# Attention output by stationary values: two heads in the halves of one bank, reciprocal sums turned and spread by small products

## The chip, the cores and the metric

The kernel runs on one core of a Trainium2 chip. The metric is the device time of one execution in microseconds (us). The engines of the core work side by side, each from its own queue, in order: TensorE (PE) multiplies matrices and writes only to PSUM, VectorE (DVE), ScalarE (ACT) and GpSimd (POOL) do the rest, and SyncE (SP) issues most of the loads. PSUM has eight banks of 128 partitions by 512 floats; the kernel uses seven as working banks and one for a convolution.

## The reference

Two layers of an encoder block on 512 tokens of 1024 features, all in float32:

```python
for l in range(DEPTH):
    x = x + 0.5 * swiglu(rms_norm(x, ffn1_norm[l]), ...)
    h = rms_norm(x, mix_norm[l])
    p = h @ w_in[l]
    attn = mla_group(...)   # 8 heads, query and key width 96, value width 64
    conv = conv_group(...)  # gate, causal depthwise conv of 31 taps on 512 channels, LayerNorm, silu
    x = x + jnp.concatenate([attn, conv], axis=-1) @ w_out[l]
    x = x + 0.5 * swiglu(rms_norm(x, ffn2_norm[l]), ...)
    x = rms_norm(x, post_norm[l])
```

In the attention each block of 128 queries sees the keys up to its own end, with a mask in steps of 64 tokens; the softmax is over the keys, and a head's output is the softmax's weights times the values:

```python
probs = jax.nn.softmax(scores, axis=-1)
outs.append(jnp.einsum('bhqk,bhkd->bqhd', probs, vs))
```

## The kernel before

Activations are kept with the features on the partitions and the 512 tokens along the free axis (x is eight tiles of 128 by 512). The large products run in three passes on split operands: each float is a rounded high part and a remainder, and `mm3` (lines 153 to 156) adds high times high, high times low and low times high. `split` (line 158) makes the two parts, the high one on ACT, the low one on DVE. The seven working banks come from `bank`, scratch tiles from `tmp` (five buffers), operands from a ring of 40 slots of 128 by 512.

A layer is FFN1, the mixer (`mix_body`), and FFN2. The mixer projects the input, builds the queries q and keys kn with the tokens on the partitions, and the values vs, four tiles of 128 tokens by 512 (eight heads of 64). Then the heads run as a software pipeline. `ORDER` lists the stages, each with its lag in steps; in a step, head (step - lag) goes through each stage:

- `turn` (line 799, lag 0) turns a head's queries and keys, so that the 96 features are on the partitions.
- `scores` (line 812, lag 1) makes the scores of four query blocks against 128, 256, 384 and 512 keys (line 825), adds the mask with a small bf16 product (line 826), takes the row maximum on DVE (line 827) and the exponential on ACT (line 831), which also leaves the row sums in `sums`: tokens on the partitions, four query blocks by two heads of a pair.
- `turn_p` (line 836, lag 3) turns the ten blocks of 128 by 128 of weights (line 846) and copies them to the ring (line 849): for each key block j a tile pt[j] with the keys on the partitions and the queries from block j to the last along the free axis.
- `values` (line 852, lag 4): for each query block t and each key block j up to t, a float32 product with the block of pt[j] stationary (128 by 128) and the head's 64 columns of vs[j] moving. The two heads of a pair share a bank; the query tokens are on its partitions. After the odd head DVE takes the reciprocals of the sums (line 864) and multiplies the bank by them (line 866), a factor for each token and head.
- `turn_out` (line 870, lag 5), for odd heads: four turns of 128 by 128 on PE (line 877) bring the pair's 128 features onto the partitions, and `split` makes one operand of the output product.

A float32 product is two matmuls in the trace; a turn is one.

The depthwise convolution runs meanwhile. Blocks 0 and 3 of its channels run on DVE (line 900), blocks 1 and 2 as products on ACT (line 904) and sums on POOL (line 908), the latter with three buffers in between. POOL then adds up the four blocks (lines 922 to 924), and PE takes the mean over the channels from that (line 926). The LayerNorm follows: DVE subtracts the mean, ACT and DVE sum the squares, PE sums over the partitions (line 192), POOL takes the inverse root (line 172), PE spreads it (line 210), DVE and ACT finish (lines 942 to 945). The output product takes four operands from the attention (`at`) and four from the convolution (`cv`); `early_groups` (line 914) does the attention's half of the first output tiles before the convolution's half is there. Four weight tiles of w_out are loaded ahead (`WOP`).

The order of each engine's queue is not the order of the program text. A planner simulates the program with its own costs of the instructions and emits each instruction when its inputs and buffers would be there, earlier program text first.

Of the kernel before, what the change touches and what calls it, by code (L numbers as in the profile page):

```python
# [7 lines left out]
FP = mybir.dt.float32  # L8
# [47 lines left out]
EVP = "DAD"  # L56
ORDER = "t0s1p3v4o5"

# [12 lines left out]
@with_exitstack  # L71
def encoder_kernel(ctx: ExitStack, tc: tile.TileContext, xT, consts, vecs, rgain, wgu1, wd1,
                   wcv, wql, wkl, wuq, wkv, wout, wgu2, wd2, wend, gend, out):
# [12 lines left out]
    def nm(s):  # L86
        uid[0] += 1
        return f"{s}{uid[0]}"
# [4 lines left out]
    def tmp(w=S, dt=FP):  # L93
        return tmps.tile([P, w], dt, tag="t", name=nm("t"))

    def bank():
        return psum.tile([P, S], FP, tag="ps", name=nm("ps"))
# [513 lines left out]
    def mix_body(kpool, l, gx, norm, done):  # L611
# [61 lines left out]


        tabs = []
        for side in range(2):
# [175 lines left out]
        def values(h):  # L852

            if h % 2 == 0:
                heads[h]["po"] = bank()
            po = heads[h - h % 2]["po"].rearrange("p (t h d) -> p t h d", t=NT, h=2)
            for t in range(NT):
                for j in range(t + 1):
                    T.matmul(po[:, t, h % 2], heads[h]["pt"][j][:, (t - j) * P:(t - j + 1) * P],  # L859
                             vs[j][:, h * DV:(h + 1) * DV], start=j == 0, stop=j == t)  # L860
            if h % 2 == 0:
                return
            rs = small.tile([P, NT, 2], FP, tag="rs", name=nm("rs"))
            V.reciprocal(rs, heads[h - 1]["sums"])
            o = tmp()
            V.tensor_tensor(o.rearrange("p (t h d) -> p t h d", t=NT, h=2), po,
                            rs[:, :, :, None].to_broadcast([P, NT, 2, DV]), ALU.mult)
            heads[h]["o"] = o

        def turn_out(h):  # L870

            if h % 2 == 0:
                return
            o = heads[h]["o"]
            ps = bank()
            for t in range(NT):
                T.transpose(ps[:, t * P:(t + 1) * P], o[:, t * P:(t + 1) * P], ident)
            at.append(split(ps))

        STAGES = [({"t": turn, "s": scores, "p": turn_p, "v": values, "o": turn_out}[c], int(d)) for c, d in zip(ORDER[::2], ORDER[1::2])]  # L880
        for step in range(H + 6):
# [277 lines left out]
```

## Time and profile before

| | before |
|---|---|
| median of three runs | 1769.82 us (1769.27 to 1770.27) |
| profiled execution | 1768.75 us |
| its span, first to last instruction | 1767.0 us |
| PE busy | 1747.5 us (99%) |
| DVE busy | 1399.8 us (79%) |
| ACT busy | 948.1 us (54%) |
| POOL busy | 266.4 us (15%) |
| line 859, values products | 320 matmuls, 39.6 us busy |
| line 877, turns of the output | 32 matmuls, 5.0 us busy |

The profiled execution is one execution recorded by the hardware's profiler; its time beside the span includes what lies around the first and the last instruction. Busy times are averages over the whole span; a matmul's recorded duration overlaps with its neighbours', so the time that a matmul holds PE is read from its start to the next one's. In the rows below a timeline gives start, duration, engine, line, operation, tiles (output, then inputs), shapes (stationary rows by columns, then the moving or the output shape), and in brackets the idle time before with what ended it. A grouped row gives the count, then busy time and mean duration in ns, then idle time and its releasers. The attention of layer 0 lies between 446 and 503 us, that of layer 1 between 1322 and 1379.

### The profile page before, as it was taken

Reading aid. Unit: us, or ns where it says so; the run is one execution under the profiler, and the core shown is the slowest. Engines: PE = TensorE matmul, PEld = TensorE weight load, DVE = VectorE, ACT = ScalarE, POOL = GpSimd, SP = SyncE. Lnnn points to the kernel's source line nnn. Section 1 sums busy time; section 2 is a strip of 40 time slices with the busy share of each in tenths; the row PEclk is TensorE's granted clock in tenths of the full one; section 3 lists DMA queues with packets and bytes.
Section 4 is the critical chain, followed back from the end, with each engine's and each line's share of the span. In section 5 each row is a group of like instructions: output and inputs, shape, how many; then the busy total and the mean of one; then the engine's idle time right before and its main releaser. Section 6 shows DMA issues by size and latency. Waiting matters only on the chain.

```text
span 1767.0 us, 22287 instructions
## 1 busy us (share of the span) xinstructions
PE 1747.5 (99%) x8166; PEld 1447.9 (82%) x8166; DVE 1399.8 (79%) x2021; ACT 948.1 (54%) x1484; POOL 266.4 (15%) x213
## 2 busy tenths in 40 slices
PE   8999999999999999999999999999999999999998
PEld 7788888888788888888888888888887888888886
DVE  8967887689869877878789778866989698678794
ACT  7535445457955544446555344444679555344453
POOL 1000000048842000000000000000578400000000
PEclk9999999999999999999999999999999999999999
DMA  9454434324225455352924445343251444444345
GB/s 294 138 178 138 153 98 138 125 78 128 52 106 132 129 159 166 102 161 85 294 86 153 134 136 162 103 136 115 73 140 26 143 105 152 162 143 144 107 135 151
DMA packets 121629, 236.72 MB, mean 134 GB/s; under 512 B 10544, under 2 KB 58032, under 8 KB 121520
## 3 DMA queue, kind: packets, MB, share of 16 engines
q1 hardware_dynamic: 117488, 222.08, 39.6%
q0 software_dynamic: 3456, 12.58, 3.9%
q8 instruction: 64, 1.05, 0.2%
q10 hardware_dynamic: 576, 0.64, 0.1%
q14 instruction: 45, 0.37, 0.1%
HBM read 207.99 MB, written 25.17 MB: 132 GB/s over the span
## 4 chain that ended last, share of the span: by engine, by line
PE 89%; DVE 3%; DMA 2%; POOL 2%; issue 2%; ACT 1%; SPq 1%; POOLq 0%; DVEq 0%; ACTq 0%
PE ps L154 28%; PE ps L156 28%; PE ps L155 28%; PE ps L859 2%; PE ps L825 2%; POOL y L908 1%; DMA fr<-in_wgu 1%; PE ps L846 1%; DMA d<-e 1%; DVE wl L241 1%; PE ps L192 0%; DMA r<-d 0%; PE ps L802 0%; PE ps L807 0%; POOL wl L149 0%
## 5 line engine op out<-in xcount | busy, mean ns | idle before, releaser
L155 PE MATMUL ps<-wl,r 128*128 128x512 f32 (+2 forms) x1434 | 548.3, 384 | 1.9 <-DVE wl L241 1.9
L156 PE MATMUL ps<-wh,r 128*128 128x512 f32 (+2 forms) x1434 | 544.4, 383 | 0.0
L154 PE MATMUL ps<-wh,r 128*128 128x512 f32 (+2 forms) x1434 | 529.1, 384 | 2.6 <-ACT wh L406 1.6
L239 ACT CAST wh<-fr 128x1024 fp32r<-128x1024 f32 x255 | 267.6, 1052 | 235.0 <-PE ps L155 111.1
L156 PE MATMUL ps<-r,wl 128*128 128x512 f32 x944 | 366.2, 390 | 0.5 <-POOL wl L149 0.5
L155 PE MATMUL ps<-r,wh 128*128 128x512 f32 x944 | 366.2, 390 | 0.0
L154 PE MATMUL ps<-r,wh 128*128 128x512 f32 x944 | 362.4, 393 | 1.3 <-ACT r L396 0.9
L241 DVE TENSOR_TENSOR wl<-fr,wh 128x1024 fp32r<-128x1024 f32 x255 | 309.9, 1218 | 50.2 <-ACT wh L239 49.6
L155 PEld LDWEIGHTS ps<-wl,r 128*128 128x128 f32 x1434 | 269.2, 188 | 55.3 <-DVE wl L241 3.7
L154 PEld LDWEIGHTS ps<-wh,r 128*128 128x128 f32 x1434 | 269.0, 188 | 54.8 <-ACT wh L406 1.9
L156 PEld LDWEIGHTS ps<-wh,r 128*128 128x128 f32 x1434 | 269.1, 188 | 51.7 <-issue 0.2
L143 ACT CAST wh<-raw 128x1024 fp32r<-128x1024 f32 (+2 forms) x142 | 139.8, 989 | 214.8 <-PE ps L155 87.7
L154 PEld LDWEIGHTS ps<-r,wh 128*128 128x128 f32 x944 | 177.1, 188 | 41.2 <-ACT r L396 2.0
L155 PEld LDWEIGHTS ps<-r,wh 128*128 128x128 f32 x944 | 177.2, 188 | 38.5 <-issue 1.4
L156 PEld LDWEIGHTS ps<-r,wl 128*128 128x128 f32 x944 | 177.2, 188 | 38.3 <-POOL wl L149 1.3
L149 DVE TENSOR_TENSOR wl<-raw,wh 128x1024 fp32r<-128x1024 f32 (+3 forms) x126 | 145.7, 1158 | 70.8 <-ACT wh L143 68.1
L908 POOL TENSOR_TENSOR y<-y,pr 128x511 f32<-128x511 f32 (+14 forms) x120 | 158.0, 1317 | 53.6 <-ACT pr L904 46.6
L338 DVE TENSOR_TENSOR fr<-fr,fr 128x1024 f32<-128x1024 f32 x112 | 136.3, 1218 | 10.8 <-DMA fr<-in_wgu 10.8
L486 DVE TENSOR_TENSOR x<-ps,x 128x512 f32<-128x512 f32 x120 | 81.6, 686 | 57.3 <-PE ps L156 56.9
L172 POOL TENSOR_TENSOR rtok<-vtok,minus_half 128x4 f32<-128x4 f32 x8 | 10.4, 1304 | 750.5 <-DVE vtok L198 750.5
L368 ACT ACTIVATE e<-e,rtok 128x256 f32<-128x256 f32 x120 | 59.8, 507 | 78.2 <-DVE e L359 77.8
L397 DVE TENSOR_TENSOR r<-r,r 128x512 fp32r<-128x512 f32 x88 | 58.2, 680 | 45.5 <-ACT r L396 45.4
(198 smaller groups left out, 1772.7 us busy)
## 6 DMA issues: line engine op xcount, KB each, us to landing
fr<-in_wgu SPq DMA_DIRECT2D x175, 512.0 KB, 4.1
raw<-in_wd SPq DMA_DIRECT2D x56, 512.0 KB, 4.5
d<-e SPq DMA_DIRECT2D x176, 128.0 KB, 3.0
r<-d SPq DMA_DIRECT2D x88, 256.0 KB, 3.7
raw<-in_wd SPq DMA_DIRECT2D x32, 384.0 KB, 4.1
raw<-in_wcv SPq DMA_DIRECT2D x16, 512.0 KB, 3.2
raw<-in_wout SPq DMA_DIRECT2D x16, 512.0 KB, 3.6
raw<-in_wgu SPq DMA_DIRECT2D x8, 512.0 KB, 8.2
```

Source lines behind the costliest of these rows:

```text
L143: A.copy(hi[:, :w], raw[:, :w])
L149: (G if kind in POOLW.split() else V).tensor_tensor(lo[:, :w], raw[:, :w], hi[:, :w].bitcast(FP), ALU.subtract)
L154: T.matmul(o, lh, rh, start=first, stop=False, skip_group_check=free)
L155: T.matmul(o, lh, rl, start=False, stop=False, skip_group_check=free)
L156: T.matmul(o, ll, rh, start=False, stop=last, skip_group_check=free)
L239: order["cast"] = A.copy(hi[:, :w], src[:, :w]).ins
L241: V.tensor_tensor(lo[:, :w], src[:, :w], hi[:, :w].bitcast(FP), ALU.subtract)
L338: V.tensor_tensor(oh, ah, bh, ALU.add)
L368: A.activation(out[j][:, :h], src[j][:, :h], AF.Silu, scale=r)
L397: V.tensor_tensor(d, d.bitcast(FP), hi.bitcast(FP), ALU.subtract)
L486: V.tensor_tensor(xm, pd.rearrange("p (a t j) -> p t a j", a=4, t=NT), xm, ALU.add)
L908: order["conv"] = G.tensor_tensor(acc[:, s:], acc[:, s:], pr[:, s:], ALU.add).ins
```

## The change

The values products are done for both heads of a pair in the odd head's step. The head's 64 columns of vs[j] are now stationary and pt[j] is moving, all its 512, 384, 256 or 128 queries at once; the even head's result goes to partitions 0 to 63 of the bank, the odd head's to 64 to 127. The bank then has features on its partitions already, so `turn_out` and its stage are gone. The factor that belongs to a token now runs along the free axis. To get it there, the reciprocal sums (128 tokens by 8) are turned on PE, copied by DVE to SBUF (8 by 128), and four small float32 products with constant 0/1 tiles of 8 by 128 (`sel`, one per query block, loaded once in each layer) spread each head's row over that head's 64 partitions in a second bank. ACT copies this bank to SBUF, DVE multiplies the values bank by it, and `split` now reads the product from SBUF instead of PSUM.

```diff
--- before.py
+++ after.py
@@ -54,7 +54,7 @@
 WOG = 3
 WOP = 4
 EVP = "DAD"
-ORDER = "t0s1p3v4o5"
+ORDER = "t0s1p3v4"
 
 VECS = [("g1", 8), ("gm", 8), ("g2", 8), ("gp", 8), ("gql", 3), ("gkl", 2),
         ("cw", 4 * CK), ("cb", 4), ("lg", 4), ("lb", 4), ("gq", 1), ("gk", 1)]
@@ -69,7 +69,7 @@
 
 
 @with_exitstack
-def encoder_kernel(ctx: ExitStack, tc: tile.TileContext, xT, consts, vecs, rgain, wgu1, wd1,
+def encoder_kernel(ctx: ExitStack, tc: tile.TileContext, xT, consts, sels, vecs, rgain, wgu1, wd1,
                    wcv, wql, wkl, wuq, wkv, wout, wgu2, wd2, wend, gend, out):
     nc = tc.nc
     PSUM = bass.MemoryType.PSUM
@@ -672,6 +672,8 @@
                 A.activation(j[:, :DR], pk[t][:, KVL:KW], AF.Square, accum_out=sspe[:, t:t + 1])
 
 
+        sel = kpool.tile([P, NT, P], FP, tag="sel", name=nm("sel"), bufs=1)
+        nc.sync.dma_start(out=sel[0:2 * NT], in_=sels)
         tabs = []
         for side in range(2):
             tb = small.tile([P, 4, NT, 16], FP, tag=f"tab{side}", name=nm("tab"), bufs=1)
@@ -852,32 +854,26 @@
         def values(h):
 
             if h % 2 == 0:
-                heads[h]["po"] = bank()
-            po = heads[h - h % 2]["po"].rearrange("p (t h d) -> p t h d", t=NT, h=2)
-            for t in range(NT):
-                for j in range(t + 1):
-                    T.matmul(po[:, t, h % 2], heads[h]["pt"][j][:, (t - j) * P:(t - j + 1) * P],
-                             vs[j][:, h * DV:(h + 1) * DV], start=j == 0, stop=j == t)
-            if h % 2 == 0:
                 return
             rs = small.tile([P, NT, 2], FP, tag="rs", name=nm("rs"))
             V.reciprocal(rs, heads[h - 1]["sums"])
+            po, R = bank(), bank()
+            T.transpose(R[0:2 * NT, 0:P], rs.rearrange("p t h -> p (t h)"), ident)
+            rT = kpool.tile([P, P], FP, tag="rT", name=nm("rT"), bufs=2)
+            V.tensor_copy(rT[0:2 * NT], R[0:2 * NT, 0:P])
+            for j in range(NT):
+                for e in range(2):
+                    T.matmul(po[e * DV:(e + 1) * DV, j * P:S], vs[j][:, (h - 1 + e) * DV:(h + e) * DV],
+                             heads[h - 1 + e]["pt"][j], start=j == 0, stop=j == NT - 1)
+            for t in range(NT):
+                T.matmul(R[:, t * P:(t + 1) * P], sel[0:2 * NT, t], rT[0:2 * NT], start=True, stop=True)
+            Rs = tmp()
+            A.copy(Rs, R)
             o = tmp()
-            V.tensor_tensor(o.rearrange("p (t h d) -> p t h d", t=NT, h=2), po,
-                            rs[:, :, :, None].to_broadcast([P, NT, 2, DV]), ALU.mult)
-            heads[h]["o"] = o
-
-        def turn_out(h):
-
-            if h % 2 == 0:
-                return
-            o = heads[h]["o"]
-            ps = bank()
-            for t in range(NT):
-                T.transpose(ps[:, t * P:(t + 1) * P], o[:, t * P:(t + 1) * P], ident)
-            at.append(split(ps))
-
-        STAGES = [({"t": turn, "s": scores, "p": turn_p, "v": values, "o": turn_out}[c], int(d)) for c, d in zip(ORDER[::2], ORDER[1::2])]
+            V.tensor_tensor(o, po, Rs, ALU.mult)
+            at.append(split(o))
+
+        STAGES = [({"t": turn, "s": scores, "p": turn_p, "v": values}[c], int(d)) for c, d in zip(ORDER[::2], ORDER[1::2])]
         for step in range(H + 6):
             for stage, lag in STAGES:
                 if 0 <= step - lag < H:
@@ -1135,10 +1131,14 @@
         tab = fn(ang.astype(np.float64)).astype(f32)
         consts[:, o:o + 64] = tab.reshape(NT, P, 16).transpose(1, 0, 2).reshape(P, 64)
     consts[:, CID:CID + P] = np.eye(P, dtype=f32)
+    sel = np.zeros((2 * NT, NT, P), f32)
+    for t in range(NT):
+        for h in range(2):
+            sel[2 * t + h, t, h * DV:(h + 1) * DV] = 1.0
 
     arrays = {
         "xT": a["x"][0].T.reshape(KD, P, S),
-        "consts": consts, "vecs": vec, "rgain": rgain,
+        "consts": consts, "sels": sel, "vecs": vec, "rgain": rgain,
         "wgu1": quarters(a["ffn1_w_gate"], a["ffn1_w_up"]), "wd1": cols(a["ffn1_w_down"][:, turns]),
         "wcv": cols(np.concatenate([ca, cg], 3).reshape(L, D, 2 * CW)),
         "wql": cols(w_in[:, :, :o1]), "wkl": rows(w_in[:, :, o1:o3]),
```

## The prediction

> **What bounds the kernel now.** I read the page's busy table first, then the windows of the attention stage of layer 0, then that stage instruction by instruction on TensorE (PE) and GpSimd (POOL), and last the chain of waits.
>
> ```profile
> span 1767.0 us, 22287 instructions
> PE 1747.5 (99%) x8166; PEld 1447.9 (82%) x8166; DVE 1399.8 (79%) x2021; ACT 948.1 (54%) x1484; POOL 266.4 (15%) x213
> PEclk9999999999999999999999999999999999999999
> ```
>
> PE is busy all the time at full clock, so time taken from PE should be time taken from the kernel. That is an average. The next rows are windows of one attention stage; their columns are PE, PE weight loads, DVE, ACT, POOL, each with its instruction count.
>
> ```profile
> core 0: us, PE busy (x) PEld busy (x) DVE busy (x) ACT busy (x) POOL busy (x), PEclk, DMA share, GB/s
> 446.25:462.00 15.75, 14.32 (x79) 9.07 (x78) 14.47 (x29) 15.75 (x39) 12.92 (x11) 1.00 0.50 103
> 462.00:484.00 22.00, 22.00 (x172) 19.19 (x171) 21.38 (x42) 21.75 (x55) 20.06 (x17) 1.00 0.01 2
> 484.00:503.40 19.40, 18.61 (x152) 16.71 (x151) 15.11 (x29) 13.00 (x30) 17.12 (x14) 1.00 0.00 1
> ```
>
> In the middle window four engines are full at once: PE 22.00 of 22.00 us, ACT 21.75, DVE 21.38, POOL 20.06. The reason is the depthwise convolution, whose taps run on DVE (two channel blocks) and on ACT with POOL (the other two) under the attention. POOL is the stiff one:
>
> ```profile
> 469.38 28.76 POOL L908 TENSOR_TENSOR y<-y,pr 128x503 f32<-128x503 f32 x22 [0.23 <-ACT pr L904]
> 498.10 1.27 POOL L922 TENSOR_TENSOR t<-r,y 128x512 f32<-128x512 f32 x1
> 499.44 1.27 POOL L923 TENSOR_TENSOR t<-t,y 128x512 f32<-128x512 f32 x1
> 500.79 1.27 POOL L924 TENSOR_TENSOR t<-t,r 128x512 f32<-128x512 f32 x1
> ```
>
> From 469.38 POOL adds 22 taps without a gap, then sums the four blocks, and is done at 500.79 + 1.27 = 502.06. The first user of that sum is the mean of the LayerNorm on PE (line 926):
>
> ```profile
> 497.17 2.34 PE L859 MATMUL ps<-r,r 128*128 128x64 f32 x20
> 499.35 0.61 PE L877 MATMUL ps<-cst,t 128*128 128x128 f32 x4
> 499.79 2.34 PE L859 MATMUL ps<-r,r 128*128 128x64 f32 x20
> 502.92 0.66 PE L877 MATMUL ps<-cst,t 128*128 128x128 f32 x4 [0.79 <-DVE t L866]
> 503.41 1.02 PE L926 MATMUL ps<-t,onesm 128*128 128x512 f32 x2
> ```
>
> PE comes to line 926 at 503.41, only 503.41 - 502.06 = 1.35 us after POOL has the sum ready. So two queues end nearly together here. From line 926 a chain of small steps leads to the first output product that uses the conv half:
>
> ```profile
> 508.81 0.69 DVE L187 TENSOR_TENSOR acc<-acc,t 128x512 f32<-128x512 f32 x1
> 509.73 0.95 PE L192 MATMUL ps<-ones,acc 128*128 128x1 f32 x8
> 512.02 0.69 DVE L206 TENSOR_TENSOR t<-cst,rtok 128x512 f32<-128x512 f32 x1 [1.15 <-POOL rtok L172]
> 513.39 1.02 PE L210 MATMUL ps<-t,ones 128*128 128x512 f32 x2
> 517.32 1.19 PE L154 MATMUL ps<-r,wh 128*128 128x512 f32 x4 [0.17 <-ACT r L160]
> ```
>
> It takes 517.32 - 503.41 = 13.91 us. PE fills it with the attention halves of four output tiles: that is all it has, since four (WOP) weight tiles are loaded and their buffers come free only when the conv halves are done. At 517.32 PE waits 0.17 us for ACT, so the chain, not PE's fill, ends this stretch.
>
> **The change, part by part, for a pair of heads** (four pairs a layer, two layers).
>
> *Removed on PE.* The probabilities were stationary: 10 products a head, each recorded as two matmuls. One head's 20 start at 497.17 and the next group starts at 499.35, so they hold PE 2.18 us (0.109 each), 4.36 a pair. The four turns of the output start at 499.35 and the next group at 499.79: 0.44 us. Together 4.80 us.
>
> *Added on PE.* Values stationary (64 columns), probabilities moving, f32, 512, 384, 256 and 128 columns for the four key blocks of a head. The nearest rows are the score products, f32 with the same moving widths:
>
> ```profile
> 446.28 0.38 PE L825 MATMUL ps<-r,r 96*128 96x128 f32 x2
> 446.50 0.19 PE L826 MATMUL ps<-mneg,mrow 128*128 128x64 bf16 x1
> 446.53 0.89 PE L825 MATMUL ps<-r,r 96*128 96x384 f32 x2
> 447.26 0.19 PE L826 MATMUL ps<-mneg,mrow 128*128 128x64 bf16 x1
> 447.29 1.10 PE L825 MATMUL ps<-r,r 96*128 96x512 f32 x2
> 448.23 0.19 PE L826 MATMUL ps<-mneg,mrow 128*128 128x64 bf16 x1
> 458.17 0.70 PE L825 MATMUL ps<-r,r 96*128 96x256 f32 x2 [0.19 <-ACT r L831]
> 458.71 0.19 PE L826 MATMUL ps<-mneg,mrow 128*128 128x64 bf16 x1
> ```
>
> From start to the next start: 0.94 us for 512 columns, 0.73 for 384, 0.54 for 256, 0.22 for 128; 2.43 a head. What a pair costs hangs on whether the two heads, which fill different columns of the array and different partitions of one bank, stream at once. No row shows two matmuls streaming together, so both ends stand: one after the other 2 x 2.43 = 4.86; at once 2.43 plus the first pass of the first product, which has no partner (0.94 / 2 = 0.47), 2.90. I take the second: the products share neither weights nor output partitions, and the code puts the two heads next to each other for each key block, so that the second pass of one meets the first of the other. The Trainium skill states that such tiles run concurrently ("TensorE: Matmul & The Clock Gate", part 3: three column tiles measured 2.38 times as fast); no run here shows it yet, and by that factor the pair would lie near 2 x 2.43 / (2 x 2.38 / 3) = 3.1 us, an estimate.
>
> The turn of the reciprocals is one matmul of 128 moving columns (0.11, a quarter of the 0.44 above). The spread is four f32 products of 128 columns, each two matmuls at 0.11: 0.88. So a pair costs 2.90 + 0.99 = 3.89 (0.91 less) at once, or 5.85 (1.05 more) one after the other. In each layer PE also loses the wait of 0.79 us at 502.92, because the scaled output is no longer turned on PE: it goes through DVE and ACT to the first group's fourth input, behind nine matmuls of other inputs.
>
> *Added on ACT, DVE, SP.* The prices come from these rows:
>
> ```profile
> L849 ACT COPY r<-ps 128x512 f32<-128x512 f32 x16 | 9.8, 610 | 0.0
> L160 ACT CAST r<-ps 128x512 fp32r<-128x512 f32 x8 | 4.7, 586 | 11.0 <-PE ps L877 11.0
> L160 ACT CAST r<-t 128x512 fp32r<-128x512 f32 x8 | 4.7, 607 | 0.0
> L866 DVE TENSOR_TENSOR t<-ps,rs 128x512 f32<-128x512 f32 x8 | 5.5, 684 | 1.7 <-PE ps L859 1.7
> L827 DVE TENSOR_REDUCE mx<-ps 128x1 f32<-128x128 f32 x16 | 4.5, 279 | 0.0
> ```
>
> ACT gets the copy of the spread sums, 0.61 us a pair, and the cast now reads SBUF (0.61 for 0.59): 2.5 us a layer. DVE gets the copy of the turned sums, bounded above by a read of 128 columns of PSUM, 0.28 a pair, 1.1 a layer; scaling and the low half keep their lengths. ACT is full in 462 to 484, where two pairs end: 1.2 us there push its products for POOL back. Ends: nothing (ACT's rows before 484 have run ahead of POOL, which adds 22 taps without a gap) and 1.2 us on POOL's end. I take 0.25, nearer to the gapless row. DVE's conv work is over by 497, five us before POOL's, and hides its 1.1; without that cover it costs 1.1 a layer. The small product that spreads waits on the DVE copy, and every PE instruction behind it waits too; the values products, 2.9 us, stand between and cover four DVE instructions. One more SP load a layer, 16 KB, goes in where SP issues a load every few us; if it had to wait for space, the weight loads behind it would be late, which I count as nothing.
>
> **The sum.** PE would come to line 926 at 503.41 - 4 x 0.91 - 0.79 = 498.98. POOL has nothing for it until 502.06. So of 4.4 us a layer only 1.35 moves the chain; the other 3 become idle PE time, since the four weight tiles give it no more fill. Later, PE reaches line 192 0.23 us and line 210 0.68 us after their inputs are done (509.50 and 512.71 by the DVE rows above), being busy with fill; with the fill done early part of this goes too, from 0 to 0.91, I take 0.35. With ACT's 0.25 the layer gains 1.35 + 0.35 - 0.25 = 1.45 us, the kernel 2.9. The profiled execution took 1768.75 (1767.0 span and 1.75 around it), so 1765.9; it lies 1.07 under the median of 1769.82, on whose scale the forecast is 1766.9, rounded to **1767**.
>
> **Rivals.**
>
> *One after the other (slower).* If the two column halves don't stream together, a pair costs 1.05 us more on PE, and PE, not POOL, comes last: 8 x 1.05 - 2 x 0.79 = +6.8 us, 1776.6. It decides from the point where PE reaches line 926 later than 503.41, which is a pair cost above 4.80 + 0.20 = 5.00 us. For it: no row shows streaming at once, and the weight loads of a head's two passes follow each other on one set of columns. If also each passage between whole-array and half-array products had to empty the array, a row prices it: a 128x512 matmul of the output product is recorded at 0.39 us but the next starts after 0.23, so 0.16 each time, four passages a pair, 5.1 us more, 1781.7. The Trainium skill states such a drain ("TensorEngine Tiling (Array Packing)", Key Properties). With the halves at once it changes nothing: 2.6 us a layer fit in PE's idle 3.
>
> ```profile
> 505.88 0.39 PE L155 MATMUL ps<-r,wh 128*128 128x512 f32 x1
> 506.10 0.39 PE L156 MATMUL ps<-r,wl 128*128 128x512 f32 x1
> 506.33 0.39 PE L154 MATMUL ps<-r,wh 128*128 128x512 f32 x1
> ```
>
> *POOL comes early too (clearly faster).* The order of every queue is planned anew, and POOL's waits for ACT before 469 could go with it. POOL is idle in 446.25 to 469.38 for some 3 us (12.92 busy of 15.75 in the first window alone). Then up to 3 us a layer more: 1761. Against it: ACT is at 15.75 of 15.75 there and gets more work.
>
> *ACT takes PE's place.* If attention steps, ready sooner on PE, push ACT's products back by the full 1.2 us, the gain is 0.5 a layer: 1769. A tail of it, with DVE's 1.1, reaches 1771.
>
> **Chances.** Forecast 0.50, its own range 1764.5 to 1769; one after the other 0.32; POOL early 0.10; ACT in PE's place 0.08. About 3.5 us (0.2%) is what a measurement tells from no change: faster means under 1766.3, slower over 1773.4. Faster: 0.18 of the forecast and 0.10; slower: 0.29 of the second case, 0.04 of the tails; same: the rest, 0.39. The range leaves out half of the early case below 1763.5 and the top of the slow case with its drains above 1780.5.
>
> **What would show it.** Right: a pair's values products hold PE about 3 us, starts of the two heads' matmuls together; PE idle some 3 us a layer before line 926 or in the fill behind it, with POOL's last add as releaser; line 926 near 502.1 relative to the same start. Wrong: 16 matmuls of a pair starting one behind the other over 4.9 us and PE still without gaps; or POOL's last add moved by more than 1 us either way.

## The result, and the profile after

The changed kernel takes 1776.85 us (median of 5 runs, 1775.73 to 1778.21), the kernel before 1769.82 (median of 5 beside it, 1769.27 to 1771.97). The ratio is 1.0033, 95% interval 1.0022 to 1.0043: slower, by some 6 us (the medians lie 7.0 apart). The forecast was 1767.0, a gain. The time lies inside the predicted range, at the number of the slower rival, but that rival's mechanism is not the cause, as will be seen. Of the executions of the kernel before beside the later runs, two at a much lower clock (2190.19 and 2959.81 us) are left out of the ratios.

The rows of the changed kernel below come from a second profile of it, taken beside further runs of before (run r1_after below: 1776.53 us, span 1773.8). Its lines are shifted: score product 827 (before 825), exponential 833 (831), copies of the turned weights 851 (849), reciprocal sums turned 861 and copied 863, values product 866 (859), spread 869, its copy on ACT 871, scaling 873 (866), mean 922 (926). First the page's busy table.

```profile
span 1773.8 us, 22015 instructions
PE 1745.1 (98%) x8014; PEld 1425.9 (80%) x8014; DVE 1405.0 (79%) x2029; ACT 953.9 (54%) x1492; POOL 268.2 (15%) x213
```

PE is busy 2.4 us less over the span than before (1747.5), DVE 5.2 more, ACT 5.8 more, and the span is 6.8 longer. So PE did lose work, and stood idle for longer than it lost. Where, the windows from the first score product of layer 0 to the mean product show. Columns as in the prediction; before comes first, then the changed kernel.

```profile
446.28:503.41 57.13, 54.92 (x401) 44.97 (x400) 50.96 (x98) 50.47 (x121) 50.07 (x41) 1.00 0.14 29
```

```profile
447.30:506.53 59.23, 52.98 (x326) 34.30 (x324) 53.24 (x101) 52.79 (x125) 51.05 (x41) 1.00 0.13 28
```

PE is busy 1.94 us less, but idle for 59.23 - 52.98 = 6.25 us where it was 57.13 - 54.92 = 2.21. DVE works 2.28 and ACT 2.32 us more. The rows of that stage that answer to the prediction's:

```profile
447.30 0.39 PE L827 MATMUL ps<-r,r 96*128 96x128 f32 x2
...
486.52 2.38 PE L866 MATMUL ps<-r,r 128*64 128x512 f32 x16
488.82 1.15 PE L869 MATMUL ps<-rT,sel 8*128 8x128 f32 x8
489.90 0.49 PE L827 MATMUL ps<-r,r 96*128 96x128 f32 x2
...
504.23 2.37 PE L866 MATMUL ps<-r,r 128*64 128x512 f32 x14 [0.82 <-DVE r L851]
506.53 1.12 PE L922 MATMUL ps<-t,onesm 128*128 128x512 f32 x2
...
517.18 1.02 PE L210 MATMUL ps<-t,ones 128*128 128x512 f32 x2
```

```profile
473.68 26.77 POOL L904 TENSOR_TENSOR y<-y,pr 128x501 f32<-128x501 f32 x20 [0.42 <-ACT pr L900]
500.41 1.27 POOL L918 TENSOR_TENSOR t<-r,y 128x512 f32<-128x512 f32 x1
501.76 1.26 POOL L919 TENSOR_TENSOR t<-t,y 128x512 f32<-128x512 f32 x1
503.10 1.60 POOL L920 TENSOR_TENSOR t<-t,r 128x512 f32<-128x512 f32 x1
```

Three things are to be seen. A pair's 16 values matmuls hold PE for 488.82 - 486.52 = 2.30 us, less than the 2.90 that the prediction took: the halves do stream at once. (The 14 at 504.23 are the rest of the last pair, whose first two stand further ahead.) POOL has the sum at 503.10 + 1.60 = 504.70, which is 57.40 after the stage began, where before it was 502.06 - 446.28 = 55.78. And PE comes to the mean another 1.83 us later still. Counted from the first score product, the three marks that the prediction used (POOL's sum, mean product, spread of the inverse root on line 210) stand so in layer 0:

| us from the first score product | POOL's sum | mean | inverse root |
|---|---|---|---|
| before | 55.78 | 57.13 | 67.11 |
| changed | 57.40 | 59.23 | 69.88 |

The loss of 69.88 - 67.11 = 2.77 us is the same in layer 1 (before 1321.84 to 1388.96, changed 1324.44 to 1394.32: 2.76). Two layers make 5.5 of the 6.8 us; 1.0 lies ahead of the first stage (447.30 against 446.28). What releases PE is told by the view of the waits, over the whole kernel; columns are the waiting engine and line, what it waited for, total us, times, longest. Before, then changed:

```profile
PE ps L825 <- ACT r L831: 1.6, 4, 0.6
PE ps L877 <- DVE t L866: 1.6, 2, 0.8
```

```profile
PE ps L827 <- ACT r L833: 8.2, 12, 1.1
PE ps L866 <- DVE r L851: 1.6, 2, 0.8
PE ps L861 <- DVE r L851: 0.8, 2, 0.4
```

PE's new idle time is a wait of the score products for the exponentials, 6.6 us more, and two smaller waits for DVE's copies of the turned weights; the wait of 1.6 us for the scaled output, which was turned on PE, is gone. It waits for no POOL add anywhere in the stage.

The first profile of the changed kernel shows one thing more. In its layer 0 the inverse root comes at 70.99, 1.11 later than above, and a pair's values products hold PE for 3.91 us instead of 2.30 (473.21 to 477.12):

```profile
473.21 3.98 PE L866 MATMUL ps<-r,r 128*64 128x512 f32 x16
```

The granted clock over these 3.91 us is 0.58, where it is 1.00 in the rest of the stage. Neither layer of the second profile has this; it comes back below.

### The profile page after: what moved, and what is told of

It is laid out like the page before. It is cut to its first block, busy times and chain, and to the rows that moved or that the text cites. A ratio compares the mean times of both kernels' runs of the same rounds, so it can differ in the third digit from the quotient of the medians.

```text
span 1773.9 us, 22015 instructions
## 1 busy us (share of the span) xinstructions
PE 1747.0 (98%) x8014; PEld 1428.1 (81%) x8014; DVE 1404.8 (79%) x2029; ACT 953.6 (54%) x1492; POOL 269.3 (15%) x213
## 4 chain that ended last, share of the span: by engine, by line
PE 87%; DVE 5%; ACT 4%; POOL 2%; issue 2%; DMA 1%; SPq 0%; POOLq 0%; DVEq 0%; ACTq 0%
PE ps L154 28%; PE ps L156 28%; PE ps L155 28%; POOL y L904 1%; ACT pr L900 1%; PE ps L866 1%; ACT r L833 1%; DVE wl L241 1%; PE ps L192 1%; DMA fr<-in_wgu 0%; PE ps L827 0%; DVE r L161 0%; DVE cv L896 0%; DMA d<-e 0%; PE ps L869 0%
```

## The experiments

In the ratios below the kernel before was run beside each on the same chip. The marks are those of the table above, in layer 0.

**The values products.** Theory: pairing saves PE its time, and moving the even head's products away from the even step opens waits for the exponentials. Rival: the pair streams badly. One run moves the products and leaves them as they were; the other keeps the change and takes the neighbours apart.

```diff
e1_move_only, against before
             if h % 2 == 0:
-                heads[h]["po"] = bank()
-            po = heads[h - h % 2]["po"].rearrange("p (t h d) -> p t h d", t=NT, h=2)
-            for t in range(NT):
...
-            if h % 2 == 0:
                 return
+            po = bank().rearrange("p (t h d) -> p t h d", t=NT, h=2)
+            for g in (h - 1, h):
+                for t in range(NT):
...
e2_one_by_one, against the changed kernel
-            for j in range(NT):
-                for e in range(2):
+            for e in range(2):
+                for j in range(NT):
```

> The kernel before with one edit: the even head's values products (probabilities still stationary, 20 matmuls, 2.18 us) wait for the odd head's step. Nothing is added or removed on any engine. Theory A (the place: the even head's products filled PE between the first two score products of an even step, where the second waits for the exponential of the first; with them gone PE idles about 1 us in each even step, and the odd step is PE-bound with a lump of 4.4 us): 2 to 4 us a layer slower, 1774 to 1778. Theory B (the new steps on ACT and DVE between values and output operand cost the time, not the place): 1769 to 1771, like before.

> The changed kernel with the two loops of the values products swapped: four products of the even head, then four of the odd one, so that no neighbours lie in different halves of the array. If the halves stream at once only when neighbours differ, the 16 matmuls hold PE 4.6 to 4.9 us in place of 2.30, with one meeting of the halves in the middle. Theory A (odd steps are PE-bound): nearly all of 8 x 2.4 us comes on top, 1788 to 1796. Theory B (ACT, DVE and POOL bound the stage throughout): under 8 us on top, 1777 to 1785.

e1: 1773.64 us, ratio 1.0016 (1.0006 to 1.0025), so the move alone costs some 2.8 us. The marks are 56.41, 58.77, 68.78: the mean product comes 1.64 later though no product changed. PE is idle for 3.30 us of that stretch where it was 2.21; the other 0.55 us are in its busy time, and no run says why. PE's rows at the place of one new wait, before and then e1:

```profile
462.07 1.29 PE L846 MATMUL ps<-cst,r 128*128 128x128 f32 x10
463.19 2.44 PE L859 MATMUL ps<-r,r 128*128 128x64 f32 x20
465.47 0.65 PE L825 MATMUL ps<-r,r 96*128 96x256 f32 x2
```

```profile
464.96 0.70 PE L825 MATMUL ps<-r,r 96*128 96x256 f32 x2 [0.92 <-ACT r L831]
```

The 256-column score product goes into the bank of the 128-column one, whose exponential ACT has to do first. Before, the even head's 20 values matmuls stood ahead of it and covered that. With them moved away PE stands, over the whole kernel, 3.4 us (6 times) where it was 1.6 (4 times). In the changed kernel, where ACT also has the copies of the spread sums in its queue, it is 8.2.

e2: 1784.43, ratio 1.0081 (1.0064 to 1.0098). A pair now holds PE for 3.86 us instead of 2.30, and where another instruction parted the heads, one head alone took 2.30:

```profile
486.37 3.93 PE L866 MATMUL ps<-r,r 128*64 128x512 f32 x16
490.23 1.15 PE L869 MATMUL ps<-rT,sel 8*128 8x128 f32 x8
...
504.32 2.37 PE L866 MATMUL ps<-r,r 128*64 128x512 f32 x8
506.62 1.15 PE L869 MATMUL ps<-rT,sel 8*128 8x128 f32 x8
```

So the second head costs no time on PE when its products alternate with the first head's, and PE's odd step is for the most part on the path: of 1.56 us a pair, 6.2 a layer, 4.90 show at layer 0's inverse root (74.78). The median rises over the changed kernel's by 7.6, each on its own chip, which is still in the range of the second theory.

**The low half from SBUF.** In the stage's rows one more thing had changed: DVE's subtraction that makes the low half (line 161) now reads two SBUF tiles. Grouped by form, before (446 to 506 us) and changed (447 to 507 us):

```profile
L161 DVE TENSOR_TENSOR r<-ps,r 128x512 fp32r<-128x512 f32 x4 | 2.8, 690 | 3.8 <-ACT r L160 3.8
```

```profile
L161 DVE TENSOR_TENSOR r<-t,r 128x512 fp32r<-128x512 f32 x3 | 4.1, 1378 | 0.5 <-ACT r L160 0.5
```

The three that fall beside POOL's adds take 1.38 us on average, the fourth, after POOL's end, takes 0.69 (at 508.08, below). The last of the slow ones has a tail on DVE:

```profile
502.12 1.46 DVE L161 TENSOR_TENSOR r<-t,r 128x512 fp32r<-128x512 f32 x1 [0.48 <-ACT r L160]
503.50 1.01 DVE L851 COPY r<-ps 128x512 f32<-128x512 f32 x2
...
508.08 0.69 DVE L161 TENSOR_TENSOR r<-t,r 128x512 fp32r<-128x512 f32 x1 [0.69 <-ACT r L160]
508.69 0.68 DVE L928 TENSOR_TENSOR r<-r,ps 128x512 f32<-128x512 f32 x1
```

The copies of the last head's turned weights (line 851) stand behind it in DVE's queue, and PE's last values products wait 0.82 us for them (504.23 above). The test scales in place, so that the split reads PSUM again:

```diff
e3_psum_out and r2_psum_out, against the changed kernel
-            o = tmp()
-            V.tensor_tensor(o, po, Rs, ALU.mult)
-            at.append(split(o))
+            V.tensor_tensor(po, po, Rs, ALU.mult)
+            at.append(split(po))
```

> The changed kernel, but DVE writes the scaled output back into its bank instead of SBUF, so ACT's cast and DVE's subtraction read PSUM as they did before the change. The subtraction takes 1.09 us in the attention of the changed kernel (two SBUF inputs while POOL adds) and 0.69 with a PSUM input in the kernel before. Theory: contention with POOL; it returns to 0.69 and POOL's last sum from 1.59 to 1.27, DVE gains 0.4 a pair, the tail 0.8 a layer: 1.5 to 3 us faster than the changed kernel, 1774 to 1775.5. Rival: the length comes from the tile being fresh, not from POOL, or the gain is hidden: 1776 to 1778.

> The changed kernel itself, on one chip with the next two, so that they share the runs of the kernel before. 5.5 to 7.5 us over it, as when it was first timed (1776.85 against 1769.82).

> The changed kernel with the output scaled in its bank, once more and beside the changed kernel. Theory: DVE's subtraction with two SBUF inputs slows down beside POOL's adds, and stands in the tail of the attention where the last pair's copy waits behind it; 3 to 5 us under the changed kernel. If the difference seen before (1772.6 on another chip) was the chip's: 0 to 2 us.

e3: 1772.55, ratio 1.0017 (1.0007 to 1.0026). Beside each other on one chip, the changed kernel took 1776.53 (1.0042, 1.0029 to 1.0055) and this one 1773.84 (1.0024, 1.0014 to 1.0034): 2.7 us. The intervals overlap a little; the marks of layer 0 say 69.88 - 68.19 = 1.69 us. The subtraction is at 0.69 again, POOL's sum at 56.38 instead of 57.40, and PE's wait for line 851 is gone:

```profile
L161 DVE TENSOR_TENSOR r<-ps,r 128x512 fp32r<-128x512 f32 x4 | 2.7, 686 | 1.1 <-ACT r L160 1.1
```

```profile
501.82 1.28 POOL L919 TENSOR_TENSOR t<-t,r 128x512 f32<-128x512 f32 x1
```

**Is POOL the lid, and what does an idle PE cost?** Three kernels without the normalisation (no division by the softmax's sums: the reciprocals, their turn, spread and scaling are left out) and one of before with its sum over the four blocks moved to DVE.

```diff
e4_no_scale, against the changed kernel
-            V.reciprocal(rs, heads[h - 1]["sums"])
-            T.transpose(R[0:2 * NT, 0:P], rs.rearrange("p t h -> p (t h)"), ident)
...
-            A.copy(Rs, R)
-            V.tensor_tensor(o, po, Rs, ALU.mult)
-            at.append(split(o))
+            at.append(split(po))
e6_no_scale_sum_on_dve (on e4) and e5_sum_on_dve (on before)
-        G.tensor_tensor(ysum, ys[0], ys[1], ALU.add)
-        G.tensor_tensor(ysum, ysum, ys[2], ALU.add)
-        (G if YP else V).tensor_tensor(ysum, ysum, ys[3], ALU.add)
+        V.tensor_tensor(ysum, ys[0], ys[1], ALU.add)
+        V.tensor_tensor(ysum, ysum, ys[3], ALU.add)
+        V.tensor_tensor(ysum, ysum, ys[2], ALU.add)
e10_no_scale_warm, on e4: small products of constants after the last turns
+        with tc.issue_after(heads[H - 1]["t"]):
+            idle(18)
```

> The changed kernel without the normalisation: no reciprocal, no turn, no spread, no copy, no scaling; the output is split straight from its bank. It leaves the division by the softmax sums out. PE loses 1.2 us a pair, ACT 0.6, DVE 1.1, and the tail loses three steps in a row (copy, scaling, cast behind it). Theory A (place of the products): PE still waits for ACT in even steps, only the odd lump and the tail shrink: 1769 to 1773. Theory B (the scaling path on ACT and DVE): all of the loss and PE's gain show, 1763 to 1767.

> The changed kernel without the normalisation (the division by the softmax sums is left out), and with the three convolution sums on DVE. Without the normalisation alone, PE came to the mean product 4.9 us before POOL's last add in both layers, idled, and the clock fell to 0.76 to 0.88 in that window. Theory C (POOL's chain is the lid on any gain of PE, and the idle time behind it costs clock too): PE's wait falls to 1 to 2 us, the clock stays, 3 to 4 us a layer come free: 1764 to 1768. Rival (something else holds that stretch): 1772 to 1774, as without this edit.

> The kernel before with one edit: the three adds that sum the four convolution blocks run on DVE in place of POOL, the block that POOL finishes last being added last. POOL's chain then ends with its last tap, some 4 us earlier, and one DVE add follows (0.7). Theory C (in the kernel before PE, not POOL, comes last to the mean product, by 1.35 us): nothing to gain, 1769 to 1771. Rival (POOL's chain ends the stage there): 2 us a layer, 1765 to 1767.

> The changed kernel without the normalisation (the division by the softmax sums is left out), and with 18 idle products on PE (128 columns, no reader) after the last head's turns, so that PE does not idle for 4.9 us before the mean product. POOL's chain is untouched. Theory D (the idle time also costs clock): the granted clock in the 14 us around the mean product is 1.00 in place of 0.88 and 0.76, the stretch from the mean product to the spread of the inverse root goes from 11.7 and 12.8 us back to 10 to 10.5, 1 to 2.5 us a layer faster than without the idle products (1773.2): 1769 to 1771.5. Rival (that stretch is bound by DVE, ACT and POOL anyway): 1772 to 1774.

e4: 1773.21, ratio 1.0018 (1.0008 to 1.0027): even without the whole normalisation the kernel is slower than before. PE now waits for POOL, 4.9 us in each layer:

```profile
502.86 1.76 PE L911 MATMUL ps<-t,onesm 128*128 128x512 f32 x2 [4.89 <-POOL t L909]
```

The marks are 56.11, 56.16, 67.88: PE could have come at about 51.3, and POOL's sum holds it. From the mean to the inverse root it takes 11.72 instead of before's 9.98, and in layer 1 12.79. The windows say why; the granted clock is the third number from the end. e4, then e10, which issues products of constants in the gap:

```profile
494.00:508.00 14.00, 9.11 (x37) 5.59 (x36) 6.80 (x12) 7.67 (x13) 8.34 (x7) 0.88 0.00 0
1372.00:1386.00 14.00, 9.11 (x32) 6.24 (x28) 5.64 (x9) 5.43 (x9) 5.84 (x5) 0.76 0.00 0
```

```profile
494.00:508.00 14.00, 13.91 (x79) 9.97 (x77) 7.52 (x13) 7.49 (x13) 8.16 (x7) 1.00 0.00 0
1372.00:1386.00 14.00, 13.88 (x77) 10.12 (x76) 7.33 (x12) 6.72 (x11) 7.41 (x7) 1.00 0.00 1
```

e10: 1767.85, ratio 0.9989 (0.9980 to 0.9998), with POOL untouched: its marks are 56.14, 56.19, 66.32. The two ways from the mean are 10.13 and 10.12 us, 4.3 less together, and the medians lie 5.4 apart (2.9 thousandths of the kernel before, each on its own chip): that is what PE's idling before line 911 cost through the clock. The Trainium skill ("TensorE: Matmul & The Clock Gate", Part 1) states that the array's clock falls to half after an idle window of some 3.4 us; the trace agrees for this gap, with an idle time of 4.89 us followed by matmuls of 0.63 us that take 0.39 otherwise. In e6 (next) and r2 (further below) the clock fell behind shorter recorded idle times than that figure; there the measurement decides.

e6: 1769.11, ratio 0.9995 (0.9985 to 1.0004). With the sums on DVE the wait falls to 2.6 us a layer, and 4 us are gained on e4. In layer 0 the mean product behind this wait takes 1.13 us, in layer 1 behind the same wait 2.07, and the way to the inverse root is 10.12 and 11.63 us: a recorded wait of 2.65 us can cost clock or not. e5: 1778.62, ratio 1.0045 (1.0030 to 1.0060), a miss: on before the sums stand in DVE's queue behind the last pair's scaling and low half, which wait for PE and ACT, and the mean came later, not earlier. It tells nothing of the lid.

**The wait for the exponentials.** Theory: more than half of a pair's values products, left in the next step, cover it. The changed products are cut into key block 0 and blocks 1 to 3, all on top of the scaling in the bank.

```diff
e7_halves, on e3: a stage of its own, a step later, for blocks 1 to 3
-ORDER = "t0s1p3v4"
+ORDER = "t0s1p3v4w5"
e8_halves_sum_on_dve: e7 with e5's sums on DVE
e9_forced_halves, on e7: held back behind a later head's first score product
+            with tc.issue_after(heads[h + 4]["s0"]) if h + 4 < H else nullcontext():
                 part(h, (1, 2, 3))
```

> The changed kernel with the scaled output kept in its bank, and the values products of a pair spread over two steps: the first key block of both heads (40% of the columns, neighbours still in different halves) in the odd step, the other three, the spread and the scaling in the next even step. Theory A (a lump of PE work in odd steps and none in even ones makes PE wait for ACT): the waits of the score products for ACT fall from 8.5 us to 3 to 5, and the time by 1 to 3 us against the same without the spreading (1772.5): 1769.5 to 1771.5, with POOL's chain then nearly last. Rival (the waits come from ACT's load): unchanged, 1772 to 1774.

> The changed kernel with the output scaled in its bank, the values products spread over two steps, and the convolution sums on DVE. If theories A and C hold, PE's saving now has neither the lump nor POOL's chain in its way: 2 to 3 us a layer under the kernel before, 1764 to 1767. If ACT's and DVE's load is the floor: 1768 to 1772.

> As the kernel with values spread over two steps, which the planner had put back into one burst; here the second part (three key blocks and the spread) must wait for the next head's first score product, so the burst is really split on PE: 512-column products in the odd step, the rest in the even one, between two score products. Theory A (lump and gap): the score products' waits for ACT fall under 5 us (8.5 with one burst), 1 to 3 us under the kernel with the output scaled in its bank. Rival (ACT's load sets those waits): no difference to it within 1 us.

e7: 1770.96, ratio 1.0008 (0.9998 to 1.0017), but the planner issued most pairs in one burst again, so it tests little. e9, really cut for the first two of a layer's four pairs: 1771.70, ratio 1.0012 (1.0002 to 1.0021), 2.1 us under r2 on the same chip, with intervals that overlap. The score products' wait falls from 8.5 to 6.0 us, not to before's 1.6, and turns and values products now wait for exponentials too, 1.9 us: 7.9 in all. The mean product now stands at 56.72, right behind POOL's sum at 56.39: the lid is reached, by 0.4 us earlier than before. The way to the inverse root, though, is 67.96 - 56.72 = 11.24.

Covering the wait is thus not all that e9 changes. In layer 0 its inverse root is 0.23 us ahead of r2's, in layer 1 it is 1.58 (67.94 for 69.52). r2's layer 1 has the stretch of the first profile again: behind waits of 0.92 and 1.10 us for exponentials a pair's values products hold PE for 4.00 us instead of 2.30. The granted clock, third from the end, of r2 in the middle of layers 0 and 1:

```profile
463.00:485.00 22.00, 19.14 (x120) 12.66 (x119) 21.77 (x43) 21.86 (x55) 19.40 (x16) 1.00 0.01 1
1340.00:1362.00 22.00, 19.38 (x116) 12.78 (x115) 21.55 (x42) 21.21 (x50) 19.33 (x17) 0.92 0.00 1
```

Both layers of e9 stand at 1.00 there. The mean granted clock of a whole execution is 0.998 or less in 4 of 5 of the changed kernel beside it (r1_after) and 8 of 9 of r2, in 2 of 11 of e9 and 5 of 23 of before. So most of e9's 2.1 us can be clock that the cut products keep; no run separates this from the wait. e8: 1779.43, ratio 1.0048 (1.0031 to 1.0065), with e5's fault.

**Behind the lid.** Two edits on e9, each alone and both: the last pair's low half on POOL (for that pair the scaling writes SBUF again), and the mean as three products that add up in the bank, so that POOL's last two sums go.

```diff
g1_last_low, on e9, for the last head
+                A.copy(hi, o)
+                G.tensor_tensor(lo, o, hi.bitcast(FP), ALU.subtract)
g2_mean3, on e9
-        G.tensor_tensor(ysum, ysum, ys[2], ALU.add)
-        (G if YP else V).tensor_tensor(ysum, ysum, ys[3], ALU.add)
-        T.matmul(pm, onesm, ysum, start=True, stop=True)
+        T.matmul(pm, onesm, ysum, start=True, stop=False)
+        T.matmul(pm, onesm, ys[3], start=False, stop=False)
+        T.matmul(pm, onesm, ys[2], start=False, stop=True)
g3_both: the two together
```

> The kernel with the output scaled in its bank and the values products forced apart over two steps, and the last pair's low part subtracted on POOL instead of DVE. In that kernel the mean product starts 0.4 us a layer earlier than before, measured from the first score product of the stage, but the spread of the inverse root follows 11.2 us later in place of 9.98: the LayerNorm's subtractions stand on DVE behind the last pair's scaling and subtraction, which wait for ACT. Theory E (that queue): the 11.2 falls to 10.3 to 10.7, 1 to 2 us in all: 1769.5 to 1771. Rival: the stretch is set elsewhere, 1771.5 to 1773.

> The same kernel (low part on DVE again), with two of POOL's three sums left out: PE takes the mean as three accumulating products, of the sum of the first two blocks, of the last DVE block and of POOL's last block. POOL's chain ends 2.7 us earlier, PE gets 1.9 us more, of which it can do 1 before POOL's last tap. Theory C (POOL's chain is the lid): the last of the mean products moves 1 to 1.5 us earlier a layer, 2 to 3 us in all: 1768.5 to 1770. Rival (PE's waits for ACT set it): PE's extra work shows, 1772 to 1775.

> Both edits together. If both theories hold, 3 to 5 us under the kernel with the split products (1771.7): 1767 to 1769, a little under the kernel before. If only one holds, what that one gives; if neither, 1772 to 1775.

g1: 1782.53, ratio 1.0066 (1.0052 to 1.0080), clearly worse: in POOL's queue the low half, which waits for ACT's cast, came to stand ahead of the last sum.

```profile
503.24 1.27 POOL L939 TENSOR_TENSOR t<-t,y 128x512 f32<-128x512 f32 x1
508.34 1.26 POOL L890 TENSOR_TENSOR r<-t,r 128x512 fp32r<-128x512 f32 x1 [3.82 <-ACT r L889]
509.56 1.26 POOL L940 TENSOR_TENSOR t<-t,r 128x512 f32<-128x512 f32 x1
```

```profile
510.87 2.08 PE L942 MATMUL ps<-t,onesm 128*128 128x512 f32 x2 [4.61 <-POOL t L940]
```

By accident it tests the lid from the other side: POOL's sum late, PE idle 4.61, then at half clock (2.08 for the 1.13 of e9). g2: 1772.12 (1.0009, 1.0000 to 1.0017); g3: 1771.53 (1.0007, 0.9998 to 1.0016). Neither can be told from e9: at e9's marks PE reaches the mean only 0.33 us after POOL, and two more products of some 0.9 us stand on the path in place of two sums.

**The last pair's tail.** In e9 the mean product starts at 503.69, and DVE's first use of it at 506.38, behind the last pair's scaling and low half, as at 508.08 in the changed kernel's rows above. The last test puts these, for the last pair, behind the LayerNorm's reduction (behind line 198 on DVE); the output product's first groups take their fourth operand later.

```diff
h1_tail_later, on e9; h2_tail_later_plain, the same on e3
-                    group(early[m], wo[m], at, range(4), KD)
+                    group(early[m], wo[m], at, range(3), KD)
         r = st.token(CW)
+        po, Rs = at.pop()
+        with tc.issue_after(st.last):
+            V.tensor_tensor(po, po, Rs, ALU.mult)
+            at.append(split(po))
+        for m in range(E3):
+            group(early[m], wo[m], at, range(3, 4), KD)
```

> The kernel with the values split over two steps and the scaling in the bank, and beside that the last pair's scaling and split put behind the LayerNorm's first reduction on DVE and ACT (the output product's first groups take their fourth operand later). In the run without this edit the mean product starts at 503.69 and DVE's first subtraction of the mean only at 506.38, behind the copy of the spread sums (0.59), the scaling (0.70), the cast (0.59) and the low half (0.69) of the last pair. Theory (this tail is what lengthens the way from the mean to the spread inverse root, 11.24 us against 9.98 in the kernel before): ACT's table load starts at about 504.4 and not 505.76, the way shrinks by 1.4 us a layer, 2.8 in all, 1768.9 us, under the kernel before. Rival (what is taken from this way comes back as a wait of PE for the fourth operand, or the POOL chain ends just as late): no change, 1771.7 us.

> The same edit on the kernel with the scaling in the bank alone, whose values products stand in one burst; without the edit it took 1772.55 and 1773.84 us. Theory: 2 x 1.2 us less (its way from mean to spread was 10.62, against 9.98), some 1771 us; the exponentials' waits of 8.5 us stay. Rival (the burst and its wait decide, the tail is hidden): 1773 us.

h1: 1769.41 us beside 1770.51 of before, ratio 0.9996 (0.9987 to 1.0005). DVE subtracts the mean as soon as it is there:

```profile
503.21 1.12 PE L937 MATMUL ps<-t,onesm 128*128 128x512 f32 x2
...
512.92 1.02 PE L210 MATMUL ps<-t,ones 128*128 128x512 f32 x2
```

```profile
504.37 0.69 DVE L943 TENSOR_TENSOR r<-r,ps 128x512 f32<-128x512 f32 x1 [2.69 <-PE ps L937]
```

The way from mean to inverse root is 9.71 us, 1.53 less than in e9, and the stage ends at 66.52 (it begins at 446.40), 0.59 before the kernel before. This was the theory's number, and it undoes the loss; no gain beyond before can be measured. h2: 1772.96, ratio 1.0010 (1.0002 to 1.0019), where the theory said 1771 and the rival 1773: the median is the rival's. Its way to the inverse root is 9.65, 0.95 less than e3's 10.60, but the mean product itself starts 504.90 - 447.25 = 57.65 after the stage's start. By the marks its inverse root is 0.89 us (layer 0) and 0.87 (layer 1) ahead of r2's; these 1.8 us can't be told from nothing in its median.

| us from the first score product, layer 0 | POOL's sum | mean | inverse root | inverse root, layer 1 | ratio |
|---|---|---|---|---|---|
| before | 55.78 | 57.13 | 67.11 | 67.12 | 1 |
| changed | 57.40 | 59.23 | 69.88 | 69.88 | 1.0042 |
| scaling in the bank (r2) | 56.41 | 57.57 | 68.19 | 69.52 | 1.0024 |
| and the products cut (e9) | 56.39 | 56.72 | 67.96 | 67.94 | 1.0012 |
| and the tail later (h1) | 56.46 | 56.81 | 66.52 | 66.54 | 0.9996 |

## Why the prediction was wrong, by its steps

**Right: the halves stream at once.** Taken was 2.90 us a pair, measured 2.30; the prediction's extra pass without a partner did not show. The drains of 0.16 us at four passages a pair, which the slower rival named, are not ruled out: the turn held PE for 0.20 to 0.29 us where 0.11 was worked out, the spread for 1.08 where it was 0.88, and the score product behind it for 0.33 where 0.22 is usual (489.90 to 490.23), some 0.4 to 0.5 us a pair against 0.64. The rule of the Trainium skill ("TensorE: Matmul & The Clock Gate", Part 3) that such tiles run concurrently holds here for two-pass float32 products: one head alone and two as neighbours take the same 2.30. So the slower rival hit 1776.6 by luck: its mechanism, one head after the other, isn't there. Even with the heads apart (e2) a pair took 3.86, not 4.86.

**Right: POOL's sum is the lid behind PE.** e4 (PE waits 4.9 us for it), e6 (the wait halves with the sums on DVE) and g1 (its delay goes to the mean) show it.

**Wrong: PE's arrival at line 926, "503.41 - 4 x 0.91 - 0.79 = 498.98".** This was the first step to fail. It subtracted PE's saved work from PE's arrival as if PE always had the next thing to do. By the measured 2.30 it should have come even earlier; it came 59.23 us after the stage's first score product instead of 52.70, 6.5 later. Of these, 4.8 are idle time: 6.25 us, where the forecast left 2.21 - 0.79 = 1.42. The other 1.7 are busy time that wasn't saved, 1.94 us in place of 4 x 0.91 = 3.64; only part of that is found, in the longer turn and spread. As to the idle time, a step named as removed had been work that stood in a place: the even head's products covered a wait for the exponentials. The prediction counted the instructions that move and not what they covered. e1 prices this at 2.8 us by itself. It explains 1.8 of the 6.6 us by which that wait grew. e4, which has the paired products without the normalisation, shows 3.4 us on the score products, as e1 does, and 0.9 on the turns. So the other 4 of the 8.2 us come only with the normalisation, by ACT's copies or by its steps on PE and DVE; no run tells which.

**Wrong: "scaling and the low half keep their lengths".** The row was there (line 161 from PSUM, 690 ns), but not for two SBUF inputs beside a busy POOL, which takes twice that; the term should have had both ends. Putting it right is worth 2.7 us by the medians on one chip (r1_after against r2_psum_out). The Trainium skill ("SBUF — State Buffer", SBUF: two separate sides) would have warned: a DVE instruction with two SBUF inputs and a GpSimd instruction that reads SBUF share a pair of ports, and the later one blocks. The trace agrees on which instructions suffer. The delay here, 0.60 to 0.77 us, is less than a whole add of 1.27, as it can be when the subtraction comes in the middle of one: that of 502.12 came 0.36 us behind the start of POOL's add of 501.76.

**Wrong: "the other 3 become idle PE time", at no price.** In the changed kernel this idle time did not arise. Where it does (e4), it costs some 4 to 5 us by the clock (e10). Had the rest gone as predicted, the gain of 2.9 could have been lost to this: e6's 2.65 us of idle time, near the 3 of the forecast, cost 11.63 - 10.12 = 1.5 us in one of its two layers.

**Wrong: the waits at lines 192 and 210 giving 0.35 a layer.** The stretch from the mean to line 210 grew by 10.65 - 9.98 = 0.67 instead, since DVE's subtraction of the mean stands behind the last pair's low half. The prediction had looked at what PE fills the stretch with, and not at the queue of DVE. h1 shows it: 1.53 us a layer against e9.

**Mis-sized: ACT's price on POOL's end, 0.25.** POOL's sum comes 1.62 later, counted from the first score product, which is more than the 1 us that the prediction named as a sign of being wrong. In layer 0, 0.3 to 0.7 is there in the runs that move the products and leave no low half in SBUF, also in e1 (56.41) and e4 (56.11), which add no copy on ACT; the other 1.0 goes with the low half from SBUF (57.40 against 56.41 in r2). So the copies on ACT are at most a small part of what pushes POOL. (In the first profile's layer 0 the sum is at 58.50: POOL stood 1.23 us for ACT at 485.89, behind the stretch at the lower clock.)

What stays open: the cut products bring the score products' wait for the exponentials to 6.0 us only, and no run separates what is left into ACT's added copies, the other steps of the normalisation and the order of the heads. Nor does one separate the loss of clock inside the attention, 1.7 us on PE where it comes, from these waits. And the shares of the three causes were measured one on top of the other, not each alone.

## What to carry to other kernels

Before an instruction is moved or shortened, look at what waits just behind it: work on a full engine may be the cover of another engine's latency, and its removal then shows as a wait in the same place. When an operand moves from PSUM to SBUF, check every reader of it for a second SBUF input beside a busy GpSimd. And where the sum of terms says that an engine will idle, follow two more things: its clock, which here fell behind several waits of about 1 us as well, and the in-order queue of each engine that the waiting step has to pass.

## What the runs showed of the hardware

Two float32 products with 64 stationary columns each, in different halves of the array, cost no more than one: 2.30 us for 1280 moving columns, alone or as a pair, and 3.86 when the two heads' products follow each other. A DVE subtraction of 128 by 512 floats took 0.69 us with an input from PSUM, and also with both from SBUF once POOL was quiet; beside POOL's adds it took 1.29 to 1.46, and POOL's last add 1.60 instead of 1.27. One idle stretch of 4.9 us on PE was followed by matmuls of 0.63 us instead of 0.39, and two such stretches cost the kernel 4.3 us by its rows, 5.4 by the medians; 18 small products of constants in each undid that. A recorded idle time of 2.65 us was followed by a mean product of 2.07 us in one layer of e6 and of 1.13 in the other. Behind waits of 0.92 and 1.10 us within 6 us the granted clock fell in one layer of r2 and not in the other, and a pair's values products took 4.00 us instead of 2.30.
